# Seven block products in place of eight for the first product of 26 feed-forward pairs, and modulation sums at larger distances in the second feed-forward network

## The chip, the cores and the metric

The kernel runs on one core of one Trainium2 chip. The metric is the time of one execution on the device in microseconds (us). Three runs of the kernel before took 1920.34, 1920.95 and 1924.17 us, so the median is 1920.95 us.

A core has these engines, by the names that the profile uses: PE (TensorE, matmuls, with PEld for its weight loads), DVE (VectorE), ACT (ScalarE), POOL (GpSimd) and SP (SyncE, which issues most transfers). Each works through its own queue in order; semaphores hold an instruction back until what it reads or overwrites is ready. SBUF is the on-chip memory; PSUM holds matmul results in eight banks of 128 x 512 numbers.

## The reference

A model of two layers runs over 256 latent tokens and 256 context tokens of width 1024. Each layer is a feed-forward network (FFN), a token mixer (gated DeltaNet in layer 0, windowed attention in layer 1) and a second FFN. So there are four FFNs; the second is the last of layer 0, the third is the first of layer 1. Everything is float32. What matters here:

```python
def _modulated_norm(h, gain, shift, scale):
    return _rms_norm(h, gain) * (1.0 + scale) + shift

def _swiglu(h, w1, w2):
    a, b = jnp.split(h @ w1, 2, axis=-1)
    return (jax.nn.silu(a) * b) @ w2
...
    for i in range(DEPTH):
        mx = (cond_x @ ada_w[i] + ada_b[i]).reshape(n_batch, 3, 3, 1, d)
        mc = (cond_c @ ada_w[i] + ada_b[i]).reshape(3, 3, d)
        x = x + FFN_RESIDUAL * mx[:, 0, 2] * _swiglu(
            _modulated_norm(x, norm_g[i, 0], mx[:, 0, 0], mx[:, 0, 1]), ffn_w1[i, 0], ffn_w2[i, 0])
        ctx = ctx + FFN_RESIDUAL * mc[0, 2] * _swiglu(
            _modulated_norm(ctx, norm_g[i, 0], mc[0, 0], mc[0, 1]), ffn_w1[i, 0], ffn_w2[i, 0])
```

The first product is `h @ w1` with a w1 of 1024 x 5632 (two halves of 2816 = 22 x 128 columns, for a and b). Shift, scale and gate come from `cond @ ada_w`, 18 vectors in all.

## The kernel before

Activations lie transposed: eight tiles `X[k]` of 128 features x 512 tokens, columns 0 to 255 the context (CTX) and 256 to 511 the latent tokens (LAT). A float32 product is made of three faster ones: every operand is split into a rounded part hi and a remainder lo (`hi` an ACT copy into the type fp32r, `lo` a subtraction on DVE or POOL), and `mm3` sums hi*hi, hi*lo and lo*hi. `H` holds hi and lo of the modulated, normalised input.

An FFN is worked in three parts of 6, 8 and 8 of its 22 column pairs (`self.parts`). A pair is 128 columns of a and the matching 128 of b. In a part, the first product of each pair fills two PSUM banks, `pa` and `pb` (`ffn1_pairs`, L1000): for each bank 8 slices of the 1024 features x 3 products of 128 x 512. Then `ffn_evac` (L872) forms `G` = silu(a) * b, again as hi and lo: silu on ACT, the product on DVE with `pb` read from PSUM, the hi copy on ACT, the lo subtraction on DVE. After its pairs a part does its second product with w2 (`out_blocks`, L1057), whose results are added to X by two `add_gated` instructions each on DVE (u<-mm,mod, 128x256). These mark the end of a part's first product in the queues. In the first part of the second and third FFN, the first two pairs go by token halves (`halves_first`, L1018) while the norm of the second half is still being made.

Weights come by transfers of 128 x 8 x 256 numbers into four buffers (two `raw`, two `ub`); `plan_weights` (L306) lists them and the units that PE uses, a unit being 8 x 128 x 128 numbers. `_split` (L447) makes hi and lo of a unit from its buffer: two ACT copies and two subtractions of 128 x 512. `w_ahead` (L483) keeps LOOK = 4 units split ahead of PE, at most one every 1000 ns of planned time.

The order in every queue is fixed when the program is built. The class `Sched` (L69) walks a planned clock: PE's products advance it, and tasks written as generators are stepped when their time has come. `note` and `product` hold its planned durations, and `at` tells a task how long its inputs will still take by them.

Beside the FFNs runs `ada_gen` (L682), the modulation sums: for each of the 16 vectors left, 16 steps, each of which fetches a 128 x 512 tile of ada_w and multiplies it by the condition. With two conditions one goes over DVE (a scalar_tensor_tensor, u<-u,cc) and the other over an ACT copy and a POOL add; with one condition the first 8 steps go over DVE and the last 8 over ACT and POOL. The steps stand at least `PACE` = 2450 ns of planned time apart. After a vector's 16 steps come a few small products on PE (ones). In the kernel before, this task ends in the middle of the third FFN.

All tensor instructions of DVE, ACT and POOL carry line L184, the wrapper in `Queue`; all matmuls carry L284. The names u, raw, ub, mm, cc and mod stand for the working tiles (76 buffers), the two weight buffers, PSUM banks, the conditions and the modulation vectors.

Of the kernel before, what the change touches and what calls it, by code (L numbers as in the profile page):

```python
# [5 lines left out]
F32 = mybir.dt.float32  # L6
F32R = mybir.dt.float32r
AF = mybir.ActivationFunctionType
ALU = mybir.AluOpType
# [5 lines left out]
F = 2816  # L15
CTX = slice(0, 256)
LAT = slice(256, 512)
# [196 lines left out]
class Kernel:  # L214
# [57 lines left out]
    def mm(self, out, lhsT, rhs, start=True, stop=True, tp=None, ns=None):  # L272
        kw = {} if tp is None else {"tile_position": tp}
# [10 lines left out]
        self.nc.tensor.matmul(out, lhsT, rhs, start=start, stop=stop, **kw)  # L284
        self.s.tick(ns)
# [6 lines left out]
    def mm3(self, ps, w, h, nk, sl=ALL, ks=None, start=True, stop=True):  # L292

        whi, wlo = w
        hhi, hlo = h
        ks = range(nk) if ks is None else ks
        for i, k in enumerate(ks):
            if h is self.H:
                self.h_wait(k, sl)
            wh, wl = whi[k // 4][:, k % 4, :], wlo[k // 4][:, k % 4, :]  # L300
            self.mm(ps[:, sl], wh, hhi[k][:, sl], start=(start and i == 0), stop=False)
            self.mm(ps[:, sl], wh, hlo[k][:, sl], start=False, stop=False)
            self.mm(ps[:, sl], wl, hhi[k][:, sl], start=False, stop=(stop and i == len(ks) - 1))


    def plan_weights(self):  # L306
# [13 lines left out]
        def unit(r, views, shape):  # L320
            for i in r:
                self.raws[i]["left"] += 1
            self.units.append({"r": r, "views": views, "shape": shape, "w": None})

        def cols(mat, r0, nk, c0, w=256):

# [6 lines left out]
        def ffn1(w1, p0, n):  # L333
# [7 lines left out]
            for p in range(p0, p0 + n, 2):  # L341
                ra = cols(w1, 0, 8, 128 * p)
                rb = cols(w1, 0, 8, F + 128 * p)
                for i in range(2):
                    std(ra, i)
                    std(rb, i)

        def rows(w2, p0, n):
# [18 lines left out]
        for l in range(2):  # L367
            for j in range(2):
                w1, w2 = a["ffn_w1"][l, j], a["ffn_w2"][l, j]
                for p0, n in self.parts:  # L370
                    if first:
                        ffn1(w1, 3, 3)
                        first = False
                    else:
                        ffn1(w1, p0, n)
                    (rows if l and j else ffn2)(w2, p0, n)
# [70 lines left out]
    def _split(self):  # L447
        un = self.units[self.u_split]
        nc = self.nc
        tiles = [self.raws[i]["tile"] for i in un["r"]]  # L450
        nk, w = un["shape"]
        hi, lo = [], []
        if w == 512:
            hi.append(self.u(dt=F32R))
# [25 lines left out]
            self.raws[i]["until"] = max(self.s.free["scalar"], self.s.free["gpsimd" if self.lo_pool or self.norming else "vector"])  # L480
        self.u_split += 1

    def w_ahead(self):  # L483

        while self.u_split < len(self.units):
            un = self.units[self.u_split]
            self._load()
            if self.u_split >= self.u_use + self.LOOK or self.urgent and self.u_split > self.u_use and len(self.hready) < 8:
                yield 200
            elif any(i >= self.r_next for i in un["r"]):  # L490
                yield 200
            else:
                t = self.at(*[self.raws[i]["tile"] for i in un["r"]])
                if t:
                    yield t
                else:
                    self._split()
                    yield 100 if self.u_split <= self.u_use + 1 else 1000

    def w_get(self, i=0):  # L500
        while self.u_split <= self.u_use + i:
# [180 lines left out]
    def ada_gen(self, todo, pace):  # L682
# [22 lines left out]
        for i, (l, v, conds, h, k) in enumerate(steps):  # L705
# [112 lines left out]
    def h_chunks(self, hf, l, slot, ks, pace=None):  # L818
# [16 lines left out]
        for k in ks:  # L835
# [10 lines left out]
            if k % 2:  # L846
# [10 lines left out]
    def norm_half(self, hf, sq, l, slot):  # L857
# [7 lines left out]
        if hf == "x":  # L865
            self.tables("silu")
            self.norming = self.urgent = self.lo_mix = False
            if (l, slot) == (0, 2):
                self.ada_pause = self.ada_hold = False


    def ffn_evac(self, pa, pb, sl):  # L872
# [4 lines left out]
        nc.vector.tensor_tensor(out=g[:, sl], in0=sa[:, sl], in1=pb[:, sl], op=ALU.mult)  # L877
        self.act(out=ghi[:, sl], in_=g[:, sl], func=AF.Copy)
        nc.vector.tensor_tensor(out=glo[:, sl], in0=g[:, sl], in1=ghi[:, sl].bitcast(F32), op=ALU.subtract)
        self.G[0].append(ghi)  # L880
        self.G[1].append(glo)

# [117 lines left out]
    def ffn1_pairs(self, n, sl):  # L1000
        for _ in range(n):
            pa, pb = self.mmt(), self.mmt()
            for ps in (pa, pb):
# [2 lines left out]
                    self.ffn_evac(pa, pb, sl)  # L1006
                self.w_done()

    def mm_narrow(self, ps, w, sl):


# [93 lines left out]

    def ffn(self, l, j, sl, nxt, start=False):
        v = 8 if j else 2
        for pi, (p0, n) in enumerate(self.parts):
            self.G = ([], [])
            if pi == 2 and (l, j) == (0, 0):  # L1110
                self.ada_hold = True
            if pi == 0:
# [3 lines left out]
                elif sl is ALL:  # L1116
                    prev = []

                    def evac(i, ps):
                        prev.append(ps)  # L1120
                        if i % 2:
                            self.ffn_evac(prev[i - 1], ps, ALL)

                    self.halves_first(4, evac)
                    self.ffn1_pairs(n - 2, sl)
                else:
                    self.ffn1_pairs(n, sl)
            else:
                self.ffn1_pairs(n, sl)
            last = pi == 2  # L1130
            if last and (l, j) == (0, 0):
                self.ada_pause = True
# [69 lines left out]
    def dn_gates(self, ps):  # L1202
# [26 lines left out]
        for e in range(2):  # L1229
            for half in range(2):  # L1230
# [750 lines left out]
    def run(self, upto=None):  # L1981
        self.upto = upto
        nc = self.nc
        self.acc = self.rs = None
        self.table = None
        self.ready = set()
        self.margin = 300.0
# [63 lines left out]
```

## Time and profile before

| | |
|---|---|
| median of three runs | 1920.95 us |
| profiled execution: time, span | 1922.17 us, 1920.4 us |
| mean granted PE clock | 0.989 |
| matmuls of 128 x 512: count, busy | 5748, 1398.0 us |
| matmuls of 128 x 256: count, busy | 2260, 348.8 us |
| last products of the modulation sums | at 1377 us |

The page gives busy times by engine over the span; a pipelined PE counts as busy between its matmuls' modelled ends. A row of the groups reads: line, engine, operation, tile written <- tiles read, shape, count, then busy us and mean ns of one, then the engine's idle time before such instructions and what ended it. A row of the timeline reads: start, length in us, engine, line, operation, tiles, shape and count of a run of like instructions. A row of the table by stretches gives the stretch, its length and the busy us (and number) of PE, PEld, DVE, ACT and POOL, the granted clock, the share of the DMA engines and GB/s.

### The profile page before, as it was taken

The page shows a single profiled execution, that of the slowest core. Times are in us where ns is not written, and L with a number is a line of the kernel's source. Part 1 is how long each engine was busy: PE and PEld are TensorE (multiplying, and loading weights), DVE is VectorE, ACT ScalarE, POOL GpSimd, SP SyncE. Part 2 cuts the span into 40 slices and gives each one's busy share as a digit, 9 for nine tenths or more (in the row PEclk, how much of TensorE's full clock was granted, in tenths as well). Part 3 has the DMA queues.
Part 4 walks back from the last instruction along what each step waited for, and adds up shares of the span by engine and source line. Part 5 has one row for each costly group of instructions (what it writes and reads, how often), then busy time and mean ns, then how long its engine had stood idle before and what let it go on. Part 6 is the DMA issues. An engine that isn't in the chain of part 4 may idle for free.

```text
span 1920.4 us, 28976 instructions
## 1 busy us (share of the span) xinstructions
PE 1861.0 (97%) x10719; PEld 1525.2 (79%) x10719; DVE 1286.5 (67%) x2124; ACT 966.7 (50%) x2106; POOL 642.2 (33%) x594
## 2 busy tenths in 40 slices
PE   7999999998999999999999999999999999899998
PEld 5878888897777666798888888888888898688887
DVE  4887877755987965578787885745433345967565
ACT  4544534456466545465444444533332348867553
POOL 3343433353546535354343342321200047330000
PEclk9999999999999998999999999999999999999999
DMA  9655554413322252344555454455323325126561
GB/s 294 217 190 188 172 175 154 129 48 123 94 58 76 67 182 83 127 159 160 192 187 191 159 178 162 138 170 190 129 88 110 110 67 122 55 67 191 193 198 66
DMA packets 238708, 271.70 MB, mean 141 GB/s; under 512 B 12343, under 2 KB 189135, under 8 KB 238567
## 3 DMA queue, kind: packets, MB, share of 16 engines
q1 hardware_dynamic: 237703, 269.15, 43.4%
q8 instruction: 84, 1.38, 0.3%
q10 hardware_dynamic: 720, 0.59, 0.1%
q14 instruction: 57, 0.47, 0.1%
q0 software_dynamic: 144, 0.11, 0.0%
HBM read 259.32 MB, written 10.49 MB: 140 GB/s over the span
## 4 chain that ended last, share of the span: by engine, by line
PE 59%; DVE 9%; ACT 3%; issue 2%; POOL 1%; DMA 0%; DVEq 0%; POOLq 0%; ACTq 0%
PE mm L284 58%; DVE u L184 7%; ACT u L184 3%; DVE big L184 1%; PE mm L289 1%; POOL u L184 1%; DVE st L184 0%; DMA u<-XD 0%; ACT ub L184 0%; DVE ub L184 0%; ACT L184 0%; DVEq L184 0%; ACT sc L184 0%; POOLq L184 0%; ACTq L184 0%
## 5 line engine op out<-in xcount | busy, mean ns | idle before, releaser
L284 PE MATMUL mm<-u 128*128 128x512 f32 (+4 forms) x9480 | 1775.5, 353 | 21.5 <-POOL u L184 9.2
L284 PEld LDWEIGHTS mm<-u 128*128 128x128 f32 (+1 forms) x9480 | 1455.9, 185 | 325.1 <-issue 42.0
L184 POOL TENSOR_TENSOR u<-u 128x512 f32<-128x512 f32 (+4 forms) x386 | 425.6, 1108 | 903.9 <-ACT u L184 863.0
L184 ACT ACTIVATE u<-u 128x256 f32<-128x256 f32 (+8 forms) x361 | 170.9, 485 | 448.7 <-DVE u L184 435.4
L184 ACT ACTIVATE u<-mm 128x128 f32<-128x128 f32 (+5 forms) x382 | 152.0, 414 | 255.9 <-PE mm L284 174.2
L184 DVE TENSOR_TENSOR u<-raw,u 128x512 fp32r<-128x512 f32 (+2 forms) x270 | 220.0, 856 | 56.0 <-ACT u L184 55.9
L184 DVE SCALAR_TENSOR_TENSOR u<-u,cc 128x512 f32<-128x512 f32 x196 | 223.5, 1141 | 8.4 <-DMA u<-in_ada_w 5.2
L184 DVE TENSOR_TENSOR u<-ub,u 128x512 fp32r<-128x512 f32 x252 | 198.7, 831 | 30.7 <-ACT u L184 30.5
L184 ACT ACTIVATE u<-raw 128x512 fp32r<-128x512 f32 (+1 forms) x372 | 206.0, 607 | 8.2 <-PE mm L284 5.2
L184 ACT ACTIVATE u<-u,cc 128x512 f32<-128x512 f32 x224 | 151.8, 712 | 111.8 <-DMA u<-in_ada_w 102.7
L184 POOL TENSOR_TENSOR u<-raw,u 128x512 fp32r<-128x512 f32 x98 | 128.9, 1339 | 146.4 <-ACT u L184 116.5
L184 ACT ACTIVATE u<-ub 128x512 fp32r<-128x512 f32 (+1 forms) x282 | 156.4, 609 | 17.3 <-DVE u L184 8.2
L184 DVE TENSOR_TENSOR u<-u,mm 128x512 f32<-128x512 f32 x66 | 45.3, 686 | 164.1 <-PE mm L284 157.7
L184 DVE TENSOR_TENSOR u<-u 128x512 fp32r<-128x512 f32 (+5 forms) x158 | 98.3, 623 | 66.6 <-ACT u L184 63.3
L184 DVE SCALAR_TENSOR_TENSOR u<-mm,mod,u 128x256 f32<-128x256 f32 x168 | 74.6, 478 | 92.2 <-PE mm L284 91.8
L184 DVE SCALAR_TENSOR_TENSOR u<-u,mod 128x256 f32<-128x256 f32 (+1 forms) x140 | 88.5, 683 | 26.5 <-ACT u L184 26.2
L184 ACT ACTIVATE u<-u,mod 128x256 fp32r<-128x256 f32 (+1 forms) x124 | 56.1, 501 | 52.6 <-DVE u L184 51.8
L184 DVE SCALAR_TENSOR_TENSOR u<-mm,cw,u 128x510 f32<-128x510 f32 (+1 forms) x96 | 71.1, 742 | 11.7 <-ACT u L184 10.0
L289 PE MATMUL mm<-ident,u 128*128 128x128 f32 (+3 forms) x361 | 56.5, 292 | 23.0 <-ACT u L184 12.4
L289 PEld LDWEIGHTS mm<-ident,u 128*128 128x128 f32 (+3 forms) x361 | 43.9, 150 | 35.8 <-ACT u L184 16.4
L184 DVE TENSOR_TENSOR u<-mm,u 128x256 f32<-128x256 f32 (+2 forms) x102 | 41.6, 420 | 36.5 <-ACT u L184 16.2
L184 DVE SCALAR_TENSOR_TENSOR u<-u,aS,mm 128x128 f32<-128x128 f32 x96 | 31.0, 344 | 22.0 <-PE mm L284 21.5
(120 smaller groups left out, 601.5 us busy)
## 6 DMA issues: line engine op xcount, KB each, us to landing
u<-in_ada_w SPq DMA_DIRECT2D x256, 256.0 KB, 5.7
ub<-in_ffn_w SPq DMA_DIRECT2D x60, 1024.0 KB, 5.3
raw<-in_ffn_w SPq DMA_DIRECT2D x58, 1024.0 KB, 5.3
raw<-in_dn_w_in SPq DMA_DIRECT2D x16, 1024.0 KB, 5.7
ub<-in_ada_w SPq DMA_DIRECT2D x12, 512.0 KB, 7.3
ub<-in_ffn_w SPq DMA_DIRECT2D x6, 768.0 KB, 4.8
raw<-in_ffn_w SPq DMA_DIRECT2D x6, 768.0 KB, 5.1
raw<-in_dn_w_out SPq DMA_DIRECT2D x4, 1024.0 KB, 5.6
```

What stands on the lines that cost most here:

```text
L184: r = f(*a, **k)
L284: self.nc.tensor.matmul(out, lhsT, rhs, start=start, stop=stop, **kw)
L289: self.nc.tensor.transpose(out, in_, self.ident[:k, :k])
```

## The change

For 8 pairs of the second FFN (every other pair of its second and third part) and 18 of the third FFN's 22 (the last two of its first part, all of the others) the first product is done as a 2 x 2 block product in seven block products. Blocks are: features in two halves of 512, columns a and b, tokens CTX and LAT. With the weight blocks A1, A2 (a) and B1, B2 (b) POOL forms S1 = B1 + B2, S2 = S1 - A1, S4 = A2 - S2 and S3 = A1 - B1. The seven weight forms A11, S1, S2, S4, S3, A12, A22 are each split into hi and lo. From the input's blocks `h_forms` makes four sums per feature slice once for each FFN, and their hi and lo (`T`). Each block product is 4 slices x 3 products of 128 x 256. Partial results are copied out of PSUM by ACT between block products (`keep`) and added by DVE in the evacuation (`fast_evac`), which is a task of its own with planned waits.

The lookahead counts a form as half a unit and may split one every 500 ns of planned time. In the second FFN the modulation's step distance is multiplied by 1.6. The gate products of the DeltaNet (`dn_gates`) are put in as soon as their input is planned ready and not 2500 ns later.

```diff
+    FAST = {(1, 0): ("----ff", "ffffffff", "ffffffff"), (0, 1): ("------", "f-f-f-f-", "f-f-f-f-")}
+    FORMS = ("A11", "S1", "S2", "S4", "S3", "A12", "A22")
...
+    def _split_form(self, un, tiles):
...
+        (a1, a2), (b1, b2) = [(t[:, 0:4, cs], t[:, 4:8, cs]) for t in tiles]
+        def put(name, x, y, op):
+            st[name] = self.u((128, 4, 128))
+            nc.gpsimd.tensor_tensor(out=st[name], in0=x, in1=y, op=op)
+        if f == "A11":
+            put("S1", b1, b2, ALU.add)
+            put("S2", st["S1"], a1, ALU.subtract)
+        elif f == "S1":
+            put("S4", a2, st["S2"], ALU.subtract)
+            put("S3", a1, b1, ALU.subtract)
+        src = {"A11": a1, "A12": a2, "A22": b2}[f] if f[0] == "A" else st[f]
+        hi, lo = self.u((128, 4, 128), F32R), self.u((128, 4, 128), F32R)
+        self.act(out=hi, in_=src, func=AF.Copy)
+        nc.vector.tensor_tensor(out=lo, in0=src, in1=hi.bitcast(F32), op=ALU.subtract)
...
-            if self.u_split >= self.u_use + self.LOOK or self.urgent and ...
+            if self.ahead() >= self.LOOK or self.urgent and ...
...
-                    yield 100 if self.u_split <= self.u_use + 1 else 1000
+                    yield 100 if self.u_split <= self.u_use + 1 else 500 if un["form"] else 1000
...
-            yield (1800.0 if i < 16 else pace) - (self.s.clock - t0)
+            yield (1800.0 if i < 16 else pace * self.ada_slow) - (self.s.clock - t0)
...
+    def h_forms(self):
+        for k in range(4):
+            x, y = self.Hf[k], self.Hf[k + 4]
+            t, v = self.u(), self.u()
+            sub(nc.vector, t[:, CTX], x[:, LAT], x[:, CTX])
+            sub(nc.vector, t[:, LAT], y[:, LAT], t[:, CTX])
+            sub(nc.gpsimd, v[:, CTX], y[:, LAT], x[:, LAT])
+            sub(nc.vector, v[:, LAT], y[:, CTX], t[:, LAT])
+            for i, z in enumerate((t, v)):
...
+                self.act(out=hi, in_=z, func=AF.Copy)
+                sub(nc.gpsimd if i else nc.vector, lo, z, hi.bitcast(F32))
...
+    def fast_pairs(self, n):
...
+            def block(out, mov, first=True):
+                hi, lo = self.w_get()
+                for k in range(4):
+                    hh, hl = mov[k]
+                    self.mm(out, hi[:, k, :], hh, start=(first and k == 0), stop=False, **kw)
+                    self.mm(out, hi[:, k, :], hl, start=False, stop=False, **kw)
+                    self.mm(out, lo[:, k, :], hh, start=False, stop=(k == 3), **kw)
+                self.w_done()
+            block(pb[:, LAT], H(0, CTX))
+            keep(ta[:, CTX], pb[:, LAT])
+            block(pa[:, LAT], T(0))
+            keep(tb[:, LAT], pa[:, LAT])
+            block(pb[:, LAT], T(1), False)
+            keep(ta[:, LAT], pb[:, LAT])
+            block(pa[:, LAT], H(1, LAT), False)
+            block(pb[:, LAT], T(2), False)
+            keep(tb[:, CTX], pb[:, LAT])
+            block(pa[:, CTX], H(1, CTX), False)
+            block(pb[:, CTX], T(3), False)
+            t = self.fast_evac(pa, pb, ta, tb)
...
+    def fast_evac(self, pa, pb, ta, tb):
...
+        nc.vector.tensor_tensor(out=ta, in0=pa, in1=ta, op=ALU.add)
+        self.act(out=ta, in_=ta, func=AF.Silu)
+        nc.vector.tensor_tensor(out=tb, in0=pb, in1=tb, op=ALU.add)
+        nc.vector.tensor_tensor(out=tb, in0=ta, in1=tb, op=ALU.mult)
+        self.act(out=ghi, in_=tb, func=AF.Copy)
+        nc.vector.tensor_tensor(out=glo, in0=tb, in1=ghi.bitcast(F32), op=ALU.subtract)
...
+        self.ada_slow = 1.6 if (l, j) == (0, 1) else 1.0
...
-        yield self.spare(self.gs)
+        yield self.at(self.gs)
```

In PE's queue, before, this is the third FFN from the second product of its first part on (ones: the last products of a modulation vector, with ident their transposes):

```order
L284 MATMUL mm<-u 128x512 x178
L284 MATMUL mm<-u,ones_87 32x512 x2
L284 MATMUL mm<-u 128x512 x16
L289 MATMUL mm<-ident,u 128x64 x4
L284 MATMUL mm<-u 128x512 x204
```

And now one fast pair of the third FFN and the start of the next (big and u hold the T blocks; the first 12 are the first block product, the last row runs into the next pair):

```order
L290 MATMUL mm<-u 128x256 x12
L290 MATMUL mm<-big,u 128x256 x6
L290 MATMUL mm<-u 128x256 x6
L290 MATMUL mm<-big,u 128x256 x6
L290 MATMUL mm<-u 128x256 x18
L290 MATMUL mm<-big,u 128x256 x3
L290 MATMUL mm<-u 128x256 x21
L290 MATMUL mm<-big,u 128x256 x3
L290 MATMUL mm<-u 128x256 x21
```

A pair's 48 matmuls of 512 columns have become 84 of 256.

In DVE's queue, before, two pairs of the third FFN's last part (u<-raw and u<-ub: lo of a weight; u<-u,mm and u<-u: the evacuation):

```order
L184 TENSOR_TENSOR u<-u,mm 128x512
L184 TENSOR_TENSOR u<-u 128x512
L184 TENSOR_TENSOR u<-raw,u 128x512 x4
L184 TENSOR_TENSOR u<-u,mm 128x512
L184 TENSOR_TENSOR u<-u 128x512
```

And now a little more than one fast pair there (u<-mm,u: the evacuation's adds from PSUM; u<-u: lo of S1 to S4, and the product and lo of the evacuation):

```order
L184 TENSOR_TENSOR u<-mm,u 128x512
L184 TENSOR_TENSOR u<-u 128x512 x4
L184 TENSOR_TENSOR u<-raw,u 128x512 x2
L184 TENSOR_TENSOR u<-u 128x512
L184 TENSOR_TENSOR u<-mm,u 128x512
L184 TENSOR_TENSOR u<-ub,u 128x512
L184 TENSOR_TENSOR u<-u 128x512
L184 TENSOR_TENSOR u<-mm,u 128x512
```

Seven lo subtractions and a longer evacuation, whose steps now stand between the subtractions, take the place of four and a closed evacuation.

In POOL's queue nothing but modulation adds stood there before; now it has, for the same part, the sums S1, S2, S4, S3 between them (u<-u: modulation adds):

```order
L184 TENSOR_TENSOR u<-u 128x512 x6
L184 TENSOR_TENSOR u<-raw 128x512
L184 TENSOR_TENSOR u<-u,raw 128x512
L184 TENSOR_TENSOR u<-raw,u 128x512
L184 TENSOR_TENSOR u<-raw 128x512
```

Four instructions for each fast pair have been added, and the modulation adds now stand among them up to the last part of the third FFN.

More of the change, by code (lines that the diff above doesn't have):

```diff
@@ L269, in tables, with mm @@
             self.nc.scalar.preload_act_table_set({"exp": "natural_log_exp_and_others", "silu": "silu_and_others"}[name])
-    def mm(self, out, lhsT, rhs, start=True, stop=True, tp=None, ns=None):
-        kw = {} if tp is None else {"tile_position": tp}
+    def mm(self, out, lhsT, rhs, start=True, stop=True, tp=None, ns=None, **kw):
+        if tp is not None:
+            kw["tile_position"] = tp
         if ns is None:
@@ L299, in mm3 @@
                 self.h_wait(k, sl)
+            elif h is self.G:
+                self.s.until(lambda: k in self.Gset)
             wh, wl = whi[k // 4][:, k % 4, :], wlo[k // 4][:, k % 4, :]
@@ L322, in unit @@
                 self.raws[i]["left"] += 1
-            self.units.append({"r": r, "views": views, "shape": shape, "w": None})
+            self.units.append({"r": r, "views": views, "shape": shape, "w": None, "form": None, "size": 1.0})
         def cols(mat, r0, nk, c0, w=256):
@@ L346, in ffn1, with ffn1mixed @@
                     std(rb, i)
+        def ffn1mixed(w1, p0, n, how):
+            for p in range(p0, p0 + n, 2):
+                r = [cols(w1, 0, 8, 128 * p), cols(w1, 0, 8, F + 128 * p)]
+                for i in range(2):
+                    if how[p + i - p0] == "f":
+                        st = {"i": i}
+                        for f in self.FORMS:
+                            unit(r, [], (4, 128))
+                            self.units[-1].update(form=f, st=st, size=0.5)
+                    else:
+                        std(r[0], i)
+                        std(r[1], i)
         def rows(w2, p0, n):
@@ L369, in plan_weights @@
                 w1, w2 = a["ffn_w1"][l, j], a["ffn_w2"][l, j]
-                for p0, n in self.parts:
+                for pi, (p0, n) in enumerate(self.parts):
                     if first:
@@ L481, in _split, with ahead @@
         self.u_split += 1
+    def _split_form(self, un, tiles):
+        nc, st, f = self.nc, un["st"], un["form"]
+        cs = slice(128 * st["i"], 128 * st["i"] + 128)
+        (a1, a2), (b1, b2) = [(t[:, 0:4, cs], t[:, 4:8, cs]) for t in tiles]
[12 more added lines that the diff above has]
+        nc.vector.tensor_tensor(out=lo, in0=src, in1=hi.bitcast(F32), op=ALU.subtract)
+        un["w"] = (hi, lo)
+        for i in un["r"]:
+            self.raws[i]["left"] -= 1
+            self.raws[i]["until"] = max(self.s.free[e] for e in ("scalar", "gpsimd", "vector"))
+        self.u_split += 1
+    def ahead(self):
+        return sum(u["size"] for u in self.units[self.u_use:self.u_split])
     def w_ahead(self):
@@ L487, in w_ahead @@
             self._load()
-            if self.u_split >= self.u_use + self.LOOK or self.urgent and self.u_split > self.u_use and len(self.hready) < 8:
+            if self.ahead() >= self.LOOK or self.urgent and self.u_split > self.u_use and len(self.hready) < 8:
                 yield 200
@@ L845, in h_chunks @@
             f = None
-            if k % 2:
+            if slot != 1 and (l, slot // 2) in self.FAST:
+                if hf == "c":
+                    self.Hf[k] = self.u()
+                self.act(out=self.Hf[k][:, sl], in_=t[:, sl], func=AF.Identity, bias=B)
+                f = self.Hf[k] if k % 2 else None
+            elif k % 2:
                 f = self.u()
@@ L879, in ffn_evac @@
         nc.vector.tensor_tensor(out=glo[:, sl], in0=g[:, sl], in1=ghi[:, sl].bitcast(F32), op=ALU.subtract)
+        self.Gset.add(len(self.G[0]))
         self.G[0].append(ghi)
@@ L1007, in ffn1_pairs, with keep @@
                 self.w_done()
+    def fast_pairs(self, n):
+        H = lambda i, sl: [tuple(p[4 * i + k][:, sl] for p in self.H) for k in range(4)]
+        T = lambda i: [tuple(p[:, 256 * (i % 2):256 * (i % 2) + 256] for p in self.T[k][i // 2]) for k in range(4)]
+        nc = self.nc
+        for _ in range(n):
+            pa, pb = self.mmt(), self.mmt()
+            ta, tb = self.u(), self.u()
+            self.s.until(lambda: len(self.T) == 4)
+            def block(out, mov, first=True):
+                kw = {} if first else {"skip_group_check": True}
+                hi, lo = self.w_get()
[5 more added lines that the diff above has]
+                self.w_done()
+            def keep(dst, src):
+                self.act(out=dst, in_=src, func=AF.Copy)
+            block(pb[:, LAT], H(0, CTX))
[10 more added lines that the diff above has]
+            t = self.fast_evac(pa, pb, ta, tb)
+            next(t)
+            self.s.add(t)
@@ L1107, in ffn @@
         v = 8 if j else 2
+        self.ada_slow = 1.6 if (l, j) == (0, 1) else 1.0
         for pi, (p0, n) in enumerate(self.parts):
-            self.G = ([], [])
+            self.G, self.Gset = ([], []), set()
+            how = self.FAST.get((l, j), ("-" * 6, "-" * 8, "-" * 8))[pi]
             if pi == 2 and (l, j) == (0, 0):
@@ L1122, in evac @@
                             self.ffn_evac(prev[i - 1], ps, ALL)
+                    self.T = []
                     self.halves_first(4, evac)
[L1125 to L1129, printed above, removed]
+                    how = how[2:]
+            if not start or pi:
+                for f in how:
+                    if f == "f":
+                        self.fast_pairs(1)
+                    else:
+                        self.ffn1_pairs(1, sl)
             last = pi == 2
```

34 lines of the change are left out of this document (33 added, 1 removed).

## The prediction

> **What bounds the kernel now.** I read the page first: busy time, the 40 slices and the chain that ended last.
>
> ```profile
> PE 1861.0 (97%) x10719; PEld 1525.2 (79%) x10719; DVE 1286.5 (67%) x2124; ACT 966.7 (50%) x2106; POOL 642.2 (33%) x594
> PE   7999999998999999999999999999999999899998
> PEclk9999999999999998999999999999999999999999
> PE 59%; DVE 9%; ACT 3%; issue 2%; POOL 1%; DMA 0%; DVEq 0%; POOLq 0%; ACTq 0%
> ```
>
> TensorE (PE) is busy in almost every slice at a granted clock of 0.9 or more, and it alone holds 59% of the chain. The table by stretches says the same of the two feed-forward networks (FFNs) that change. The rows below run from the last gated add of one part of an FFN to the first of the next part, so each is one "first product" with what PE does until the second product's first result. In order they are: second FFN, second and third part; third FFN, first, second and third part. The columns are busy us (and instructions) of PE, PEld, DVE, ACT and POOL, then the clock.
>
> ```profile
> 934.20:1028.70 94.50, 94.50 (x428) 76.34 (x427) 73.47 (x85) 45.09 (x80) 35.64 (x25) 1.00 0.54 186
> 1068.60:1163.70 95.10, 95.10 (x431) 76.83 (x430) 72.24 (x84) 41.44 (x73) 33.30 (x22) 1.00 0.53 180
> 1209.40:1282.60 73.20, 72.40 (x395) 60.74 (x394) 41.73 (x63) 36.69 (x72) 20.09 (x16) 1.00 0.46 149
> 1312.00:1407.30 95.30, 95.30 (x422) 76.47 (x422) 41.36 (x63) 35.66 (x64) 13.06 (x9) 1.00 0.45 151
> 1446.20:1537.80 91.60, 91.60 (x406) 75.85 (x405) 31.53 (x51) 25.49 (x46) 0.00 (x0) 1.00 0.33 106
> ```
>
> PE never stops in four of these five. VectorE (DVE) stands at 73 of 94 us where modulation sums run beside the FFN, and at 31 to 41 of 92 to 95 us in the third FFN. So work taken from PE here shortens the run, until DVE with its neighbour GpSimd (POOL) becomes the bound.
>
> **What PE saves.** Pure runs of one shape give the spacing of matmuls, with the mean time of one beside them.
>
> ```profile
> 1389.61 30.76 PE L284 MATMUL mm<-u 128*128 128x512 f32 x135
> L284 PE MATMUL mm<-u 128*128 128x512 f32 x135 | 30.8, 389 | 0.0
> 1569.78 10.48 PE L284 MATMUL mm<-u 128*128 128x256 f32 x86
> L284 PE MATMUL mm<-u 128*128 128x256 f32 x103 | 12.5, 283 | 0.0
> ```
>
> Without the last one's own length, 512 columns come every (30.76-0.389)/134 = 0.2266 us and 256 columns every (10.48-0.283)/85 = 0.1200 us. Half of 0.2266 is 0.113, so cutting matmuls in two costs 6%. A pair was 2 x 8 x 3 = 48 of the wide ones, 10.88 us. It becomes 7 blocks x 4 x 3 = 84 of the narrow ones, 10.08 us. That is 0.80 us less a pair, and over 8 + 18 = 26 pairs **20.8 us less** on PE. The weight loads under the narrow ones are of the same shape as now, so they bring no price of their own.
>
> [...]
>
> **What DVE and POOL get.** These are rows of the second FFN's second part, where POOL works, and of the third FFN's last part, where POOL is silent, then two DVE runs inside POOL's three instructions.
>
> ```profile
> L184 DVE SCALAR_TENSOR_TENSOR u<-u,cc 128x512 f32<-128x512 f32 x26 | 31.4, 1207 | 1.5 <-DMA u<-in_ada_w 1.0
> L184 DVE TENSOR_TENSOR u<-ub,u 128x512 fp32r<-128x512 f32 x18 | 19.2, 1108 | 0.0
> L184 DVE TENSOR_TENSOR u<-raw,u 128x512 fp32r<-128x512 f32 x16 | 12.1, 800 | 2.6 <-ACT u L184 2.6
> L184 DVE TENSOR_TENSOR u<-u,mm 128x512 f32<-128x512 f32 x8 | 5.5, 685 | 9.3 <-PE mm L284 9.3
> ...
> L184 POOL TENSOR_TENSOR u<-u 128x512 f32<-128x512 f32 x24 | 35.6, 1484 | 60.4 <-ACT u L184 59.5
> ...
> L184 DVE TENSOR_TENSOR u<-raw,u 128x512 fp32r<-128x512 f32 x18 | 11.4, 684 | 0.0
> L184 DVE TENSOR_TENSOR u<-ub,u 128x512 fp32r<-128x512 f32 x16 | 10.1, 685 | 0.0
> L184 DVE TENSOR_TENSOR u<-u,mm 128x512 f32<-128x512 f32 x8 | 5.5, 688 | 52.4 <-PE mm L284 52.4
> ...
> 969.20 1.29 DVE L184 TENSOR_TENSOR u<-ub,u 128x512 fp32r<-128x512 f32 x2
> 970.40 3.50 DVE L184 SCALAR_TENSOR_TENSOR u<-u,cc 128x512 f32<-128x512 f32 x2
> 973.83 2.38 DVE L184 TENSOR_TENSOR u<-ub,u 128x512 fp32r<-128x512 f32 x2
> 976.64 0.75 DVE L184 SCALAR_TENSOR_TENSOR u<-u,cc 128x512 f32<-128x512 f32 x1
> 970.36 4.70 POOL L184 TENSOR_TENSOR u<-u 128x512 f32<-128x512 f32 x3 [5.12 <-ACT u L184]
> ```
>
> With POOL silent a 128x512 two-tensor DVE instruction takes 0.685 us, and back to back 1.29-0.685 = 0.605 us; the modulation step takes 0.75, so about 0.67 back to back. Beside POOL the same forms rise to 1.108, 0.800 and 1.207. The excess is 18 x 0.42 + 16 x 0.116 + 26 x 0.457 = 21.3 us for 24 POOL instructions: **each POOL instruction costs DVE 0.89 us**. The lower end is nothing, if POOL falls where DVE idles. The upper end is POOL's whole 1.48 us, if the two exclude each other. I stay by the row of 0.89 and take 0.81, since two of a fast pair's eleven DVE instructions, its adds from PSUM, need not be slowed: the product that reads PSUM (u<-u,mm) has 0.685 beside POOL and 0.688 without.
>
> A fast pair needs seven lo subtractions on DVE instead of four, and an evacuation of two PSUM adds, one product and one subtraction instead of a product and a subtraction. On POOL it adds four sums S1 to S4, where it had none. Counting the rows in order between the same gated adds:
>
> - Third FFN, second part: 74 + 16 two-tensor instructions, 7 modulation steps and 2 short ones on DVE are 90 x 0.605 + 7 x 0.67 + 1 = 60.2 us. POOL has 37, since five sums of the first pairs come earlier: 37 x 0.81 = 30.0. DVE needs 90.2 us; PE, at 95.3 - 8 x 0.8 = 88.9, waits about 1 us.
> - Third part: the same 60.2 on DVE with 35 on POOL, 88.6 us; PE has 91.6 - 6.4 and some 1.5 of modulation products that came earlier before, 86.7. About 2 us.
> - First part: only two fast pairs, but the H sums and their lo halves join, and the modulation runs with two conditions here now. DVE has 49 wide two-tensor instructions (29.6 us), 17 modulation steps (11.4) and 28 instructions of 256 columns, at 0.48 - 0.08 = 0.40 by the row below (11.2), some 53 us with the short ones. POOL has the worth of 32 wide instructions, 26 us: 79 against 73.2 - 1.6 = 71.6. About 7.5 us.
> - Second FFN, second and third part: with one step in 3.9 us of planned time instead of 2.45, 70 x 0.605 + 16 x 0.67 + 1.5 = 54.6 on DVE and 34 x 0.81 = 27.5 from POOL, 82 against 94.5 - 3.2 = 91. PE keeps its lead, and the 3.2 us each are kept. Its first part has no fast pair; the H sums (some 16 DVE instructions, 6 us) are hidden by the modulation steps that leave it, and cost up to those 6 us if they are not.
>
> ```profile
> L184 DVE SCALAR_TENSOR_TENSOR u<-mm,mod,u 128x256 f32<-128x256 f32 x168 | 74.6, 478 | 92.2 <-PE mm L284 91.8
> ```
>
> DVE gives back 1 + 2 + 7.5 = 10.5 us.
>
> **The other edits.** ACT (ScalarE) gets seven hi copies instead of four and four copies of half a bank.
>
> ```profile
> L184 ACT ACTIVATE u<-mm 128x256 f32<-128x256 f32 x56 | 21.1, 380 | 49.4 <-PE mm L284 48.4
> ...
> L184 ACT ACTIVATE u<-raw 128x512 fp32r<-128x512 f32 x16 | 9.1, 617 | 0.0
> ...
> ACT u L184 <- DVE u L184: 36.1, 8, 5.9
> ```
>
> The first row is of the groups by shape of the whole run; the others are of the second FFN's second part, the last one ACT's waits there (us, times, longest). The copies add a wait: PE may write a bank again one block after the copy could start, and a block is 12 x 0.12 = 1.44 us against 0.38. I cost it at nothing. If ACT is held up by more than about a microsecond, by a hi copy that waits for POOL's sum or by a silu that waits for DVE's add, the copy stands behind it and all of PE behind the copy. ACT's seven copies take 7 x 0.62 and the rest about 3 us, 7.3 of 10.08 us. The H sums and T blocks run in the first part beside ordinary pairs; their DVE time is in the sums above.
>
> The slower modulation sums move each vector's last products later: by 32 matmuls for the first of them in the second FFN, and the last vector from before the third FFN's last part into it. Every consumer still stands behind it in each queue, and the fetches on SP are the same 256. The rest of the moved step's work goes with it: its DVE half, its ACT product and POOL add are what fills the third FFN's counts above. The earlier start of the gate products in the DeltaNet is worth nothing that I can see: its queues hold other work there.
>
> **Sum.** The profiled execution took 1922.17 us, 1.2 above the median of the three runs. 1922.2 - 20.8 + 10.5 = 1911.9, or **1910.7** beside the median.
>
> **The rivals.**
> - *All is hidden.* POOL's sums run while DVE idles (price 0). Then only the 20.8 stay: 1900. For it: ACT and POOL have room. Against: DVE is close to full in three sections.
> - *No change.* DVE's price is 0.89 to 1.0 and PE also waits some tenths of a us in each pair for copies: 10 us more than my sum, 1921.
> - *ACT holds PE up: slower.* In order, ACT takes the hi copy of a POOL sum, then a PSUM copy that PE waits for. If in each fast pair one POOL instruction (1.48 us in the row) is late through to PE, it costs 26 x 1.48 = 38.5 against 20.8, while DVE's shortage hides under it: 1938. It decides from 0.8 us a pair. For it: ACT now waits 36.1 us for DVE in eight pairs, up to 5.9 at once, which costs nothing only because PE needs no ACT result within a pair. Against: the weight forms are made eight ahead, 11.5 us.
> [...]
>
> [...]
>
> **How the numbers follow.** Forecast (1903 to 1917) 0.38, all hidden 0.17, no change 0.15, ACT 0.25, ports 0.05. About 0.2%, 3.8 us, is what a measurement of this kernel can tell from no change. Faster is the first two, 0.55; same 0.15; slower 0.30. The range leaves out the ports, half of the ACT case's upper side and the last of the hidden case: 1898 to 1937. The likeliest case's own range is 1903 to 1917.
>
> **What would show it.** Right: 256-wide runs at 0.120 us, PE idle in the third FFN's first parts of some 10 us in all and released by DVE; DVE above 90% there. Wrong: PE idle released by ACT within fast pairs (the third rival), or a stretch of the second FFN longer than its 91 us. The third FFN's three stretches should come at about 79, 90 and 89 us, the second FFN's two at 91 to 92.

## The result, and the profile after

| | before | after |
|---|---|---|
| median of four runs | 1920.64 us | 1973.95 us |
| lowest to highest | 1918.38 to 1924.17 | 1972.36 to 1976.45 |
| ratio, 95% interval | | 1.0277, 1.0257 to 1.0297 |

The change makes the kernel 53 us slower. Here are the busy times, three rows of the slices and the chain, from the page of the changed kernel.

```profile
span 1974.7 us, 31559 instructions
PE 1862.7 (94%) x11655; PEld 1568.3 (79%) x11655; DVE 1483.2 (75%) x2285; ACT 1059.9 (54%) x2320; POOL 839.1 (42%) x715
PE   7999999989999999998999898799899899899998
DVE  5887867666969756697987977989969844967565
PEclk9999999999999999998999999899999999999999
PE 16%; DVE 4%; ACT 2%; issue 1%; POOL 0%; DVEq 0%; POOLq 0%; ACTq 0%
```

The chain's shares add up to 23% of the span only, so nothing is read from it. The slices say where to look: from the 19th to the 35th PE falls to 7 or 8 tenths seven times, where it had 9 before in all but one, and DVE stands at 8 or 9 in most of these. DVE has 197 us more than before, POOL 197 as well. The waits over the whole run name the releasers (us in all, times, longest):

```profile
PE mm L290 <- ACT u L184: 57.2, 36, 9.4
PE mm L290 <- DVE u L184: 15.6, 15, 5.9
PE mm L290 <- POOL u L184: 10.8, 16, 1.2
```

The table by stretches shows the same six first products as the prediction, now in the order second FFN, first to third part, then third FFN, first to third part (the columns are those of the prediction).

```profile
825.00:906.10 81.10, 73.12 (x391) 61.37 (x391) 68.44 (x83) 45.30 (x87) 40.62 (x31) 0.95 0.46 153
936.30:1030.90 94.60, 92.17 (x559) 82.25 (x558) 83.72 (x92) 51.29 (x98) 44.20 (x28) 0.98 0.45 150
1071.50:1169.60 98.10, 90.92 (x558) 80.74 (x557) 84.49 (x92) 49.68 (x95) 47.07 (x29) 1.00 0.44 145
1218.40:1310.90 92.50, 73.59 (x449) 65.45 (x450) 85.06 (x98) 52.11 (x102) 53.48 (x38) 0.91 0.41 131
1343.70:1446.90 103.20, 93.34 (x705) 88.40 (x705) 96.24 (x101) 61.16 (x124) 63.62 (x39) 0.97 0.50 162
1485.90:1590.10 104.20, 93.63 (x706) 88.71 (x705) 94.14 (x102) 55.42 (x114) 56.07 (x34) 0.97 0.43 140
```

Together they last 574 us, 60 more than the prediction has for them: 8.7, 3.3, 6.2, 13.5, 13.2 and 15.2 in this order. The stretches between them cost 8 us more than before, and the DeltaNet's first stretch took 376 in place of 383 us. The last two rows show DVE busy for 96 of 103 and 94 of 104 us: it is close to full there, as forecast, but at a higher need. PE's waits, however, end mostly with ACT, in these two rows all of them (20.4 us).

The timeline of the third FFN's first part, at the longest of these waits, shows how both are true. Its rows come engine by engine: PE, DVE, POOL, ACT; the bracket is the idle time before and its releaser.

```profile
1271.26 0.51 PE L290 MATMUL mm<-u 128*128 128x256 f32 x2 [2.32 <-DVE u L184]
1281.12 1.22 PE L290 MATMUL mm<-big,u 128*128 128x256 f32 x4 [9.36 <-ACT u L184]
...
1272.81 1.75 DVE L184 SCALAR_TENSOR_TENSOR u<-u,cc 128x512 f32<-128x512 f32 x1
1274.48 1.74 DVE L184 TENSOR_TENSOR u<-ub,u 128x512 fp32r<-128x512 f32 x1
1276.15 1.74 DVE L184 SCALAR_TENSOR_TENSOR u<-u,cc 128x512 f32<-128x512 f32 x1
1277.81 0.68 DVE L184 TENSOR_TENSOR u<-u,mm 128x512 f32<-128x512 f32 x1
...
1269.26 6.42 POOL L184 TENSOR_TENSOR u<-u 128x512 f32<-128x512 f32 x4 [5.06 <-ACT u L184]
1275.64 1.70 POOL L184 TENSOR_TENSOR u<-ub 128x512 f32<-128x512 f32 x1
1277.42 1.60 POOL L184 TENSOR_TENSOR u<-u,ub 128x512 f32<-128x512 f32 x1
...
1278.52 0.63 ACT L184 ACTIVATE u<-u 128x512 fp32r<-128x512 f32 x1 [6.14 <-DVE u L184]
1279.06 0.70 ACT L184 ACTIVATE u<-u,cc 128x512 f32<-128x512 f32 x1
1279.67 1.13 ACT L184 ACTIVATE u<-ub 128x512 fp32r<-128x512 f32 x2
1280.71 0.36 ACT L184 ACTIVATE u<-mm 128x256 f32<-128x256 f32 x1
```

Read it from the end. PE starts when ACT has copied a half bank (1280.71 + 0.36). That copy stands in ACT's queue behind the hi copy of an evacuation, which waits 6.14 us for DVE's product (u<-u,mm). The product stands behind DVE instructions that take 1.74 us each beside POOL; it reads PSUM and takes 0.68 itself. So POOL's neighbourhood makes DVE late, DVE holds ACT, and ACT's copy holds PE.

The evacuation there is that of an ordinary pair. In the third FFN's second and third part, where all pairs are fast, 10 of PE's 13 waits for ACT (16.4 of the 20.4 us) end with a copy that stands right behind a silu (u<-u in f32), and the silu has waited for DVE's add. One of them (PE, DVE, ACT):

```profile
1371.61 0.62 PE L290 MATMUL mm<-u 128*128 128x256 f32 x3 [2.99 <-ACT u L184]
...
1368.27 1.75 DVE L184 TENSOR_TENSOR u<-ub,u 128x512 fp32r<-128x512 f32 x1
1369.94 0.68 DVE L184 TENSOR_TENSOR u<-mm,u 128x512 f32<-128x512 f32 x1
...
1370.66 0.63 ACT L184 ACTIVATE u<-u 128x512 f32<-128x512 f32 x1 [3.97 <-DVE u L184]
1371.19 0.37 ACT L184 ACTIVATE u<-mm 128x256 f32<-128x256 f32 x1
```

### The profile page after: what moved, and what is told of

Same layout as the page of the kernel before. It is cut to its first block, busy times and chain, and to the rows that moved or that the text cites. A ratio compares the mean times of both kernels' runs of the same rounds, so it can differ in the third digit from the quotient of the medians.

```text
span 1974.7 us, 31559 instructions
## 1 busy us (share of the span) xinstructions
PE 1862.7 (94%) x11655; PEld 1568.3 (79%) x11655; DVE 1483.2 (75%) x2285; ACT 1059.9 (54%) x2320; POOL 839.1 (42%) x715
## 5 line engine op out<-in xcount | busy, mean ns | idle before, releaser
L290 PE MATMUL mm<-u 128*128 128x512 f32 (+4 forms) x9948 | 1727.6, 338 | 42.6 <-ACT u L184 23.8
L290 PEld LDWEIGHTS mm<-u 128*128 128x128 f32 (+2 forms) x9948 | 1447.3, 187 | 300.3 <-issue 41.4
L184 POOL TENSOR_TENSOR u<-u 128x512 f32<-128x512 f32 (+4 forms) x401 | 451.1, 1132 | 671.6 <-ACT u L184 637.6
L184 ACT ACTIVATE u<-u 128x512 fp32r<-128x512 f32 (+8 forms) x501 | 255.2, 524 | 435.6 <-DVE u L184 402.4
L184 DVE TENSOR_TENSOR u<-u 128x512 fp32r<-128x512 f32 (+5 forms) x315 | 273.2, 882 | 61.2 <-ACT u L184 54.9
L184 ACT ACTIVATE u<-mm 128x128 f32<-128x128 f32 (+4 forms) x460 | 175.7, 394 | 264.7 <-PE mm L290 190.5
L184 POOL TENSOR_TENSOR u<-raw,u 128x512 fp32r<-128x512 f32 (+1 forms) x110 | 149.0, 1375 | 145.2 <-ACT u L184 105.5
L184 DVE TENSOR_TENSOR u<-mm,u 128x256 f32<-128x256 f32 (+2 forms) x154 | 76.6, 506 | 34.7 <-PE mm L290 17.1
L290 PE MATMUL mm<-big,u 128*128 128x256 f32 x468 | 76.8, 292 | 26.4 <-ACT u L184 26.4
L290 PEld LDWEIGHTS mm<-big,u 128*128 128x128 f32 x468 | 65.7, 198 | 28.9 <-ACT u L184 28.8
```

Source lines behind the costliest of these rows:

```text
L184: r = f(*a, **k)
```

## The experiments

Theory P: a POOL instruction beside DVE costs DVE about a microsecond, so the sums S1 to S4 fill DVE. Its rivals are given with each run. Single times are of one run; ratios are to the kernel before on the same chip.

**Is it POOL's load or the wait for POOL's results?** In the first run only `src` changes, in the second the four `put` lines go too.

```diff
-        src = {"A11": a1, "A12": a2, "A22": b2}[f] if f[0] == "A" else st[f]
+        src = {"A11": a1, "A12": a2, "A22": b2, "S1": b1, "S2": a1, "S4": a2, "S3": b2}[f]
```

> The four sums S1 to S4 of each fast pair are still computed on POOL, but the weight forms named after them are taken from blocks of the raw tile, so no copy on ACT and no subtraction on DVE waits for POOL (the output is not the reference's). Theory P (port): the time is lost because each POOL sum stretches a DVE instruction beside it, so DVE is full; its load is unchanged here, so 1965 to 1977 us. Rival D (dependency): ACT's hi copies stand waiting for POOL's sums and the PSUM copies behind them; that wait is gone, so 1925 to 1940 us.

> As the run with unused sums, and POOL does not compute S1 to S4 either (output not the reference's). Theory P: the 104 sums are gone as DVE's neighbours, the third FFN's second and third first products fall from 103 and 104 us to 87 to 90 and its first from 92 to 80 to 85; 1925 to 1940 us. Rival D: the same 1925 to 1940, but then the run with unused sums is there already. If both stay above 1960, neither: the added work of ACT and DVE itself, or the H sums, hold PE.

With unused sums 1972.16 us, with no sums 1929.67. The wait for POOL's results is worth 2 us, no more than the spread between runs of the changed kernel, and POOL's presence 42.5. The second and third part came as expected; the third FFN's first, expected at 80 to 85 us, only fell to 89.4. Two rows of the table by stretches of the run without sums, the third FFN's second and third part:

```profile
1325.70:1415.10 89.40, 89.01 (x706) 85.26 (x705) 72.37 (x103) 61.33 (x124) 19.91 (x13) 1.00 0.57 187
1454.00:1543.40 89.40, 88.96 (x706) 85.46 (x705) 68.72 (x103) 56.24 (x114) 11.41 (x7) 1.00 0.48 161
```

DVE does as many instructions as in the changed kernel (103 for 101 and 102) in 23.9 and 25.4 us less, for 26 and 27 POOL instructions less: **0.92 and 0.94 us a POOL instruction**. By form, in the second part, first the changed kernel and then the run without sums:

```profile
L184 DVE TENSOR_TENSOR u<-u 128x512 fp32r<-128x512 f32 x36 | 40.0, 1136 | 1.5 <-ACT u L184 1.4
L184 DVE TENSOR_TENSOR u<-raw,u 128x512 fp32r<-128x512 f32 x18 | 17.3, 993 | 0.6 <-ACT u L184 0.6
L184 DVE TENSOR_TENSOR u<-ub,u 128x512 fp32r<-128x512 f32 x12 | 15.5, 1303 | 1.7 <-ACT u L184 1.7
L184 DVE TENSOR_TENSOR u<-mm,u 128x512 f32<-128x512 f32 x16 | 10.8, 678 | 0.0
```

```profile
L184 DVE TENSOR_TENSOR u<-ub,u 128x512 fp32r<-128x512 f32 x28 | 25.4, 928 | 5.8 <-ACT u L184 4.3 <-issue 1.0
L184 DVE TENSOR_TENSOR u<-raw,u 128x512 fp32r<-128x512 f32 x30 | 20.8, 716 | 8.5 <-ACT u L184 8.4
L184 DVE TENSOR_TENSOR u<-mm,u 128x512 f32<-128x512 f32 x16 | 10.9, 680 | 0.0
L184 DVE TENSOR_TENSOR u<-u 128x512 fp32r<-128x512 f32 x8 | 7.7, 960 | 0.1
```

The lo subtractions, with both inputs in SBUF, are 66 in both (a form's source is named raw or ub in the second run). They fall from 72.8 to 53.9 us together, 1.10 to 0.82 each, with the 13 modulation adds still on POOL; an add that reads PSUM has 0.68 in both.

**Are the copies the loss?** Each `keep` reads a tile in SBUF in place of the bank.

```diff
-                self.act(out=dst, in_=src, func=AF.Copy)
+                self.act(out=dst, in_=self.T[0][0][0][:, 0:256].bitcast(F32), func=AF.Copy)
```

> The four copies of half banks in each fast pair read a tile in SBUF in place of the bank in PSUM, so ACT does the same work but PE is not held by it within a pair (output not the reference's). Theory P: DVE is full, so PE waits as long for the weight forms as it did for the copies: 1962 to 1975 us, and PE's idle time is released by DVE or by hi copies. Rival C (copy wait, the rival of the prediction): PE's waits behind the copies are the loss itself, so 1915 to 1940 us.

1956.69 us: between the two, so neither expectation held. The gain of 17 us lies where DVE still has room: the second FFN's second and third part go from 94.6 and 98.1 to 90.1 and 91.3, the third FFN's third from 104.2 to 97.3. Its second part, with DVE busy for 98.4 us, stays at 102.3. The copy wait is real, but it is the smaller part, and without POOL's sums it costs little: the run without them kept every copy and took 89.4 us there.

**The sums on DVE.**

```diff
-            nc.gpsimd.tensor_tensor(out=st[name], in0=x, in1=y, op=op)
+            nc.vector.tensor_tensor(out=st[name], in0=x, in1=y, op=op)
```

> S1 to S4 are computed on DVE in place of POOL. Theory P: a DVE instruction with POOL silent takes 0.605 us back to back, against 1.09 us that a POOL sum costs DVE in the trace of the changed kernel, so DVE's need in the third FFN's second part falls from 102 to about 60 + 32 x 0.605 + 5 x 1.09 = 85 us, under PE's 87: 1925 to 1940 us in all, slower than the kernel before by up to 1%, since the first parts keep the H sums. Theory that DVE's own instructions are the bound (whoever does the sums): DVE has more of them now, 1965 us or more.

1939.19 us, ratio 1.0091 (1.0072 to 1.0111): as theory P has it, 35 us come back though DVE now does 104 instructions more. DVE's need fell less than expected: in the third FFN's second part it is busy for 89.1 us, not 85, and the part takes 93.4. The 1.09 us of this expectation and the next is near the price in the timelines (1.74 less 0.68); over a whole part the run without sums gives 0.92 to 0.94.

The next run moves the rest too, the modulation's second half and POOL's part of the H sums (`quiet` is true in the second and third FFN).

```diff
-                if (conds.index(cd) if len(conds) == 2 else h):
+                if not self.quiet and (conds.index(cd) if len(conds) == 2 else h):
...
-            sub(nc.gpsimd, v[:, CTX], y[:, LAT], x[:, LAT])
+            sub(nc.vector, v[:, CTX], y[:, LAT], x[:, LAT])
...
-                sub(nc.gpsimd if i else nc.vector, lo, z, hi.bitcast(F32))
+                sub(nc.vector, lo, z, hi.bitcast(F32))
```

> In the second and third FFN everything that POOL did beside the pairs is done on DVE: S1 to S4, the modulation's second half (now steps of DVE in place of an ACT product and a POOL add), and POOL's part of the H sums. Theory P (a POOL instruction costs DVE more, 1.09 us, than the same work done on DVE, 0.61 to 0.67 us): against the run with the sums on DVE (1939 us) the second FFN's first part falls from 81 to 73 to 75 us, the third FFN's first from 92 to 78 to 84, its second from 93 to 89 to 91; 1905 to 1922 us. Rival (DVE's own number of instructions is the bound now): 1935 us or more.

1937.17 us, 1.0093 (1.0076 to 1.0109): the time came as the rival has it. The second FFN's first part fell to 77.2 us only and the third FFN's second stayed at 93.7. The third FFN's first stayed at 92.7 us, with DVE busy for 80.9 in 139 instructions, and PE waiting 10.0 us for DVE and 9.5 for ACT. But DVE is idle for 12 us of it, so its number of instructions is not shown to be the bound. At PE's longest wait, 8.3 us up to 1268.51, DVE does eight modulation steps in one go (5.38 us from 1262.47) before the subtractions that PE needs: it is late at that place, with POOL silent too.

**The small edits.** The gates' edit alone on the kernel before, and the changed kernel with the modulation at its old distance:

```diff
-        yield self.spare(self.gs)
+        yield self.at(self.gs)
```

> The kernel before with one part of the change alone: the gate products of the DeltaNet are planned when their input is ready, 2.5 us of spare time taken away. The DeltaNet's first stretch went from 382.8 to 375.9 us in the trace of the changed kernel. If this edit did it: 1912 to 1916 us. Rival: the 7 us belong to another part of the change or to the chip's state, 1919 to 1923 us.

1915.82 us, 0.9977 (0.9966 to 0.9989): a gain of 2 to 7 us, that I had put at nothing.

```diff
-        self.ada_slow = 1.6 if (l, j) == (0, 1) else 1.0
+        self.ada_slow = 1.0
```

> The changed kernel with the modulation sums at their old distance in the second FFN, 2.45 us in place of 3.92. Theory P: the same POOL adds and DVE steps fall in the second FFN, where DVE (88.8 of 94.5 us) has little room, and leave the third; what one gains the other loses: 1964 to 1986 us. Rival: the steps that the slower distance pushed into the third FFN are the loss there: its first part falls to 80 us or less and the whole to 1945 to 1960 us.

1967.87 us. The second FFN's second and third part grew to 109.1 and 108.3 us, the third FFN's three shrank to 83.0, 99.7 and 89.9: 24.7 lost and 27.3 gained. The larger distance moves the load, as theory P has it.

**What holds the first parts?** The sums of H are left out of the run with S1 to S4 on DVE, then the larger distance starts one part later as well.

```diff
-        T = lambda i: [tuple(p[:, 256 * (i % 2):256 * (i % 2) + 256] for p in self.T[k][i // 2]) for k in range(4)]
+        T = lambda i: H(i // 2, LAT if i % 2 else CTX)
```

> The run with S1 to S4 on DVE for all 26 fast pairs (1939 us), with the sums and differences of H left out: the T blocks read H instead (output not the reference's). Theory H: these sums, begun while the norm's end and the modulation still fill DVE, are the loss of the first parts; second FFN's first part 81 to 72 to 74 us, third FFN's first 92 to 76 to 82; 1915 to 1926 us. Rival M (the modulation with two conditions and the forms for the next pairs fill DVE there anyway): the third FFN's first part stays above 86 and the whole at 1929 us or more.

```diff
         for pi, (p0, n) in enumerate(self.parts):
+            self.ada_slow = 1.6 if (l, j) == (0, 1) and pi else 1.0
```

> The run with the H sums left out (output not the reference's), whose second FFN's first part still took 80.0 us, with one more change: the larger distance of the modulation steps begins with that FFN's second part instead of its first. Theory N: in the first part the gate vector of layer 0 is needed by the first gated add; at 3.92 us a step four of its steps are still open then and are forced in one go, and PE's sums over partitions wait 5 us for them. With the old distance the vector is ready in time: that part takes 72 to 74 us. Rival: something else in that part holds PE, 79 to 81 us. The whole is then 1917 to 1925 against 1926 us, the later parts may shift.

Without the H sums 1926.42 us: the third FFN's first part went from 91.7 to 84.8, but the second FFN's only to 80.0. Neither expectation held: the sums of H are a part of the loss in the third FFN's first part (6.9 us), and not what holds the second FFN's. With the later start 1919.62, and the second FFN's first part takes 72.4 us, as before the change. The timeline of the changed kernel shows what was wrong (PE, DVE and POOL):

```profile
894.91 1.04 PE L290 MATMUL mm<-u,ones 128*32 128x512 f32 x2
901.81 1.93 PE L290 MATMUL mm<-u,ones 128*32 128x512 f32 x6 [5.86 <-DVE u L184]
...
894.93 6.83 DVE L184 SCALAR_TENSOR_TENSOR u<-u,cc 128x512 f32<-128x512 f32 x4
...
894.93 6.27 POOL L184 TENSOR_TENSOR u<-u 128x512 f32<-128x512 f32 x4 [4.40 <-ACT u L184]
```

The first gated add needs layer 0's last gate vector. Four of its steps are still open and run in one go, 1.7 us each beside POOL, while PE's sums over partitions wait. The run at the old distance, which keeps the H sums, has the same wait (6.3 us) and 80.7 us, and the runs below without either have 72.4: either edit alone delays the vector enough.

**Fast pairs only where DVE has room.** The third FFN's second and third part alone, the old distance, and S1 to S4 on DVE, on POOL, and on DVE with the modulation there on DVE too:

```diff
+    FAST = {(1, 0): ("------", "ffffffff", "ffffffff")}
```

> Fast pairs only where DVE has room: all 16 pairs of the third FFN's second and third part, none elsewhere, modulation at its old distance, S1 to S4 on DVE. Theory P: DVE needs about 60 + 19 + some 9 POOL adds at 0.92 = 87 us at most in the second part and less in the third, so these take 88 to 90 and 87 to 88 us in place of 95.3 and 91.6; the H sums fit into the first part, where DVE had 42 of 73 us; with the gates edit 1902 to 1912 us, faster than the kernel before. Rival H (the H sums delay the first part whatever DVE does, as 8.7 us in the second FFN): 1912 to 1920 us.

> The same 16 fast pairs alone with the sums on POOL, as in the changed kernel. Theory P at 0.92 us a POOL instruction: DVE needs 60 + 41 x 0.92 = 98 us in the third FFN's second part, which takes 98 to 104 us, and about 85 in the third, which takes 87 to 92; 1916 to 1930 us, and slower than the run with the sums on DVE by 10 to 20 us. Rival (the sums' place does not matter once the modulation is spread as before): within 4 us of that run.

> The run with fast pairs in the third FFN's second and third part alone (1907 us), and there the modulation's second half as steps on DVE, so that POOL is silent in the third FFN but for its own part of the H sums. Theory P at 0.92 us for a POOL add against 0.61 to 0.67 for the step on DVE: the second part's DVE need falls by 10 x 0.28, 3 us, and the part from 91.9 to 88 to 91; 1903 to 1908 us in all. Rival: DVE's queue in order is what delays PE there, and more instructions in it do harm: 1908 to 1914 us.

| | time, us | ratio (95% interval) | third FFN's parts, us |
|---|---|---|---|
| sums on DVE | 1907.34 | 0.9931 (0.9919 to 0.9943) | 73.6, 91.9, 85.2 |
| sums on POOL | 1921.92 | 1.0001 (0.9992 to 1.0011) | 73.8, 100.4, 89.8 |
| modulation on DVE too | 1902.94 | 0.9917 (0.9901 to 0.9934) | 73.6, 90.6, 85.2 |

The third FFN's second part in the table by stretches, with the sums on DVE and then on POOL:

```profile
1305.20:1397.10 91.90, 89.68 (x706) 85.15 (x705) 86.87 (x131) 58.93 (x121) 17.20 (x10) 1.00 0.50 158
```

```profile
1307.80:1408.20 100.40, 92.23 (x706) 87.28 (x705) 94.38 (x102) 60.35 (x124) 61.57 (x37) 0.98 0.45 145
```

DVE has 29 instructions more and is busy for 7.5 us less: 27 POOL instructions at 0.93 less 29 at 0.605. The first two came out in time as expected, but the parts with the sums on DVE took 91.9 and 85.2 us where 88 to 90 and 87 to 88 were expected. Rival H fell, since the H sums cost the first part 0.4 us where DVE had room. The third came out at the lower edge of its range, but its interval overlaps the first's, and the second part shows 1.3 us of gain, less than the 3 us of DVE's need. The first and the third row are faster than both kernels. Both hold the gates' edit too, which alone had a ratio of 0.9977; so the fast pairs of the first row are worth about 9 of its 14 us.

## Why the prediction was wrong

- **PE's saving was right.** The third FFN's last part, in the run with 16 fast pairs and the sums on DVE, had no shortage and took 85.2 in place of 91.6 us: 6.4, eight times the 0.80 us a pair. In the changed kernel the narrow matmuls come every 0.120 us too where PE doesn't wait (21 in 2.68 us); the waits hide what they save.
- **The price of a POOL instruction failed.** I had 0.89 and took 0.81, because two of a fast pair's eleven DVE instructions read PSUM (two elevenths off would be 0.73; how 0.81 follows isn't shown). They are unhurt, but the price came out at 0.92 to 0.94 all the same. For the third FFN's second part the silent share was right, 72.37 - 13 x 0.92 = 60.4 against 60.2; 39 x 0.92 brings DVE to 96.2 in place of 90.2. In the third part it is 94.1 in place of 88.6.
- **That PE waits only for what DVE lacks failed too.** The two stretches last 7 and 10 us longer than DVE is busy. I had costed the copies at nothing and given the wait behind ACT to a rival at 38.5 us. Freeing the copies gave 17, of which 11 in the second FFN, where the wait ate the 3.2 us that I let each part keep. Both signs of being wrong that I named are there: waits within fast pairs that ACT ends, and parts of the second FFN longer than 91 us. The rival had the releaser right, and one of its two ways: the silu that waits for DVE's add stands before the `keep` copy in most waits of the third FFN's last two parts, as at 1370.66 above. The other way, a hi copy that waits for POOL's sum, is worth 2 us; the hi copy that holds the `keep` copies up at 1278.52 waits for DVE's late evacuation. What makes DVE late is POOL's load, 42.5 us.
- **The first parts failed.** The third FFN's took 92.5 where I had 79. DVE was busy for 85.1, and the longest wait alone is 9.4 us. The modulation pushed there by the larger distance is worth 9.5 (92.5 to 83.0 at the old distance), the H sums 6.9 in the run with the sums on DVE (91.7 to 84.8). The second FFN's I had as unchanged, or up to 6 us longer by the H sums; the later modulation vectors I let cost nothing, because "every consumer still stands behind it in each queue". That is so, and it is the loss: the consumer of the gate vector stands at a fixed place in PE's queue and waits there. The part took 81.1 in place of 72.4.
- **The gate products** gave 2 to 7 us, not nothing. Which work in the DeltaNet waited for them wasn't tried.
- **The clock had no term.** By the estimate in the last section PE's half clock after its waits costs some 15 us in the changed kernel, on top of the waits themselves.
- **The rivals.** Nearest to the time came the upper end of the price that I named, POOL's whole 1.48 us: 1.48 less 0.81 is 0.67, for the 104 sums 70 us more, minus slack an estimate of about 1975. In the chances it is called ports, with 0.05; no run shows a port. That its time fits is luck: the whole 1.48 us was too high, and the time was reached with 0.92 to 0.94, the waits in order behind it and the clock. In the prediction's rows at 970 us DVE finished about three instructions within POOL's 4.70 us, one for each of POOL's, where at 0.605 back to back nearly eight would fit. Where DVE has only instructions with two SBUF inputs, as in the timelines, it does one of them, 1.7 us, for each of POOL's. That the adds and products that read PSUM and POOL's pauses bring the price down over a whole part is likely, but no run shows it. So for each POOL instruction DVE lost 1.74 less 0.68, 1.06 us, in the timelines and 0.92 to 0.94 over a part, in neither the whole 1.48. What stays open is how the rest of the loss divides among the waits: the parts overlap, and freeing one uncovers the next. No run put the `keep` copies ahead of the silu or hi copy in ACT's queue, so what another order would save is open too.

## What to carry to other kernels

Before work is given to an idle GpSimd beside a busy VectorE, price it by what it takes from VectorE: here a sum on POOL cost DVE 0.92 us and the same sum on DVE 0.61. Where PE's next step hangs on a result that passes two in-order queues, as here, it can stop before the helper engine is full, so take the excess of that engine's need over PE's as a lower bound of the wait: two parts here lasted 7 and 10 us longer than DVE was busy. A background task with a fixed consumer may be slowed only as far as that consumer allows.

## What the runs showed of the hardware

After its longest wait PE's clock was at 0.50. Four rows of the changed kernel's third FFN around the 9.4 us wait (the clock is the third column from the end):

```profile
1270.00:1275.00 5.00, 0.51 (x2) 0.30 (x2) 5.00 (x4) 2.38 (x5) 4.92 (x4) 0.83 0.15 47
1275.00:1280.00 5.00, 0.00 (x0) 0.00 (x0) 4.30 (x4) 1.48 (x3) 4.84 (x4) 0.50 0.00 0
1280.00:1285.00 5.00, 3.88 (x18) 3.88 (x19) 5.00 (x5) 3.90 (x10) 3.74 (x3) 0.50 0.25 65
1285.00:1290.00 5.00, 5.00 (x36) 5.00 (x36) 5.00 (x8) 2.92 (x6) 1.61 (x2) 0.80 0.32 97
```

PE resumed at 1281.1 at a granted 0.50, and the five us from 1285 have 0.80 on average, so the full clock came back at about 1287, 6 us after the wait.

A shorter wait had a low clock behind it too. The first row holds the last 2.7 us of the wait of 2.99 us up to 1371.61, and the second is the stretch behind it. The next is the sum over all nine stretches at 0.50 between 800 and 1600 us, each of which begins in a wait of PE of 1.96 to 9.36 us or within 1.6 us of its end; the kernel before had a mean clock of 1.00 there. Then come 18 narrow matmuls at 0.50 and 18 at the full clock.

```profile
1368.89:1372.30 3.41, 0.69 (x5) 0.69 (x6) 3.41 (x5) 1.64 (x5) 2.25 (x2) 1.00 0.00 0
1372.30:1375.71 3.41, 3.41 (x18) 3.41 (x17) 3.41 (x3) 0.57 (x2) 2.89 (x2) 0.50 0.02 5
...
sum 47.77, PE 35.05 PEld 30.38 DVE 39.97 ACT 23.15 POOL 28.43; mean PE 3.90 PEld 3.38 DVE 4.44 ACT 2.57 POOL 3.16
...
1282.57 4.04 PE L290 MATMUL mm<-u 128*128 128x256 f32 x18
1294.58 2.32 PE L290 MATMUL mm<-u 128*128 128x256 f32 x18
```

Not every wait of this length did it: the one of 2.67 us up to 1097.14 left the clock at 1.00. The matmuls take 4.04 in place of 2.32 us, so of the 35 us that PE worked at 0.50 an estimated 15 are lost to the clock. These waits of PE thus cost more than their length.
